# Counting TensorE's instruction blocks in a kernel's planning layer, and other PSUM buffers for two blocks of a projection

## The chip, the core and the metric

The kernel runs on one core of a Trainium2 chip. A core has a matrix engine (TensorE, PE in the profile, its weight loads PEld), a vector engine (DVE), a scalar engine (ACT), GpSimd (POOL) and SyncE (SP), which here only issues transfers. The engines run side by side, each through its own list of instructions in order, and wait for one another by semaphores. Matrix products land in PSUM; everything else lives in SBUF. The metric is the device time of one execution in microseconds.

## The reference

One decoder layer for 512 tokens of width 1024, in float32. The input is RMS-normed and projected; the projection is cut into three groups of heads, whose outputs are merged by one output projection, and a SwiGLU block follows. The change lies in the projection and in the second group, a gated linear recurrence (HGRN2):

```python
h = rmsnorm(x, norm_mix[l])
proj = h @ w_in[l]
c_q, c_kv, k_rope, hq, hf, hi, hg, mq = [proj[..., offsets[j]:offsets[j + 1]] for j in range(len(IN_SIZES))]
...
q = jax.nn.silu(q_raw.astype(f32)) * (HG_DK ** -0.5)
f = lbf + (1.0 - lbf) * jax.nn.sigmoid(f_raw.astype(f32))
k = 1.0 - f
...
x = x + (mix @ w_out[l]).astype(x.dtype)
h2 = rmsnorm(x, norm_ffn[l])
x = x + ((jax.nn.silu(h2 @ w_gate[l]) * (h2 @ w_up[l])) @ w_down[l]).astype(x.dtype)
```

## The kernel before

**Products in three passes.** An operand is split into a rounded high part and the rest (`split`, L487: ACT makes `hi`, DVE makes `lo`), and `mm3` (L517) sums three matmuls, high by high, high by low, low by high. Each of the three is one weight load and one matmul in the fp32r type: two instructions in TensorE's list. Weights come by transfer into a raw tile `wr` (three of them, `load`, L495) and are split by `piece` (L502) into `wh` and `wl` (five and four tiles).

**The order is planned.** `body` (L409) does not issue instructions; it records them with a `Recorder` (L47). `price` (L185) gives each one an estimated duration in ns. `run` (L242) then simulates the five engines: it takes again and again the operation that can start first (ties by priority), notes its end, releases what waited for it, and keeps the order in which it took them. A few copies and memsets may go to either of two engines, and `run` picks the one that ends first. `issue` (L363) emits the recorded operations in that order, with no times in it. So a price changes the order of instructions and the choice of an engine for some of them, and nothing else: on the chip each engine runs its list as soon as its semaphores allow.

**PSUM buffers.** A buffer is one bank of 128x512 float32: three are named `mm`, three `at`, two `tr`. A new product takes a buffer of its name that is free, and its first matmul waits, if it must, until the buffer's last reader is done.

**The stretch around the change.** `hg_in(h)` (L712) for heads 0 to 3 calls `gated` (L701) twice, for projection blocks 5+h and 9+h: `feat` (L624) sums 8 x 3 matmuls of 128x512, then DVE multiplies by `RX` (the norm's factor, spread over a tile; z) and ACT takes the sigmoid. Blocks 5 and 9 have their weights early and are computed interleaved, as pieces of the input arrive; blocks 6, 10, 7, 11, 8 and 12 follow with weights from `wr`. `RX` exists only when all of x has arrived and its squares have been summed. Then come the value projections (`wide`, L727, with `wva` and `wvb`), and between their matmuls the intra-chunk scores of the recurrence, in `hg_levels` (L776): a first `scores` (L783) on the raw q and k, then one per level m = 1, 2, 4, 8, 16, each after DVE has multiplied q, k and the totals up a level (`step_up`, L831), and each masked into a tile by `copy_predicated` (`put`, L793). One `scores` is 64 matmuls of a 32x32 corner of the array in plain float32; TensorE runs each as two loads and two matmuls, so 256 instructions of a few ns each. In the trace these are the instructions of L380; all others are of L383. The q and k of level m are written over in place once `scores` has read them.

Later stretches: the latent attention and the memory attention, the output projection, and the SwiGLU block in three column groups.

Of the kernel before, what the change touches and what calls it, by code (L numbers as in the profile page):

```python
# [9 lines left out]
F32R = mybir.dt.float32r  # L10
I32 = mybir.dt.int32
U8 = mybir.dt.uint8
AF = mybir.ActivationFunctionType
# [33 lines left out]
class Recorder:  # L47
# [137 lines left out]
    def price(self, o, outs, ins):  # L185
        n = max(self._free(a) for a in outs)
        if o.name == "dma_start":
            return 1000 if o.eng == "gpsimd" else 475
        if o.eng == "tensor":
            if o.name == "tiles":  # L190
                return 270 + 2.1 * sum(max(35, self._free(p[2])) for p in o.kw["parts"]) / len({self._rng(p[0])[2] for p in o.kw["parts"]})
            if o.name == "transpose":
                return 109.5
            if ins[0].dtype == F32R:
                return n / 2.4 + (15.5 if n >= 512 else 14) if n >= 256 else max(1.67 * n, 107)
            return 222 if n <= 2 else 64 if n <= 32 else 122 if n <= 64 else 226 if n <= 128 else 436 if n <= 256 else 1.7 * n
        m = max([self._free(a) for a in ins] + [n])
        fast = self.inside(ins)
        if o.eng == "scalar":
            fn = o.args[2] if o.name == "activation" else None  # L200
            if fn is not None:
                o.table = self.TABLES.get(str(fn).split(".")[-1])
            return (92 if fast else 45) + 0.835 * m + (190 if "accum_out" in o.kw else 0) + (100 if hasattr(o.kw.get("scale"), "ap") else 0)
        if o.eng == "vector":
            if o.name == "reciprocal":
                return 70 + 6.6 * m
            if o.name == "tensor_copy":
                return 66 + (0.55 if fast else 1.045) * m
            if o.name == "tensor_scalar":
                return 66 + (0.62 if fast else 1.045) * m + 60 * any(hasattr(a, "ap") for a in o.args[2:])  # L210
            if o.name == "memset":
                return 60 + 0.5 * m
            if o.name == "scalar_tensor_tensor":
                return 68 + 1.15 * m
            return 68 + 1.045 * m
        if o.name == "memset":
            return 40 + m * 0.8
        if o.name == "tensor_scalar":
            return 244 + 0.84 * m
        return 170 + 2.17 * m  # L220

    def shares(self, o, outs, ins):
# [12 lines left out]
        ("scalar", "scalar"): 135, ("scalar", "vector"): 140, ("scalar", "tensor"): 202, ("scalar", "gpsimd"): 200, ("scalar", "sync"): 130,  # L235
        ("gpsimd", "gpsimd"): 105, ("gpsimd", "vector"): 75, ("gpsimd", "scalar"): 75, ("gpsimd", "tensor"): 215, ("gpsimd", "sync"): 130,
    }


    IDLE = (1500, 3400)  # L240

    def run(self):  # L242
# [18 lines left out]
                    cand[e].append(o)  # L261
        table, dma, done, out, port, cold = None, 0.0, 0, [], 0.0, 0.0
        busy = {e: 0.0 for e in engs}
        while done < len(ops):
            best = None
            for e in engs:
                be = None
                for o in cand[e]:
                    t = max(free[e], o.ready)
                    if o.alts[e][5]:  # L270
                        t = max(t, port)
                    ok = True
                    if o.new:
                        need = {}
                        for k in o.new:
# [12 lines left out]
                            t = max(t, sorted(free_)[skip + j])  # L288
# [3 lines left out]
                    t = max(t, free[e])  # L292
# [33 lines left out]
            if o.eng == "tensor":  # L326
                if t - free["tensor"] > self.IDLE[0] or not free["tensor"]:
                    cold = t + self.IDLE[1]
                slow = min(2 * cost, max(0.0, cold - t))
                cost += slow / 2  # L330
            end = t + cost
            if both:
                port = end
# [2 lines left out]
            if o.dma:  # L336
                ap = o.kw["out"]
# [71 lines left out]
def body(ctx, tc, t):  # L409
# [14 lines left out]
    def nm(p):  # L424
        cnt[0] += 1
        return f"{p}_{cnt[0]}"
# [6 lines left out]
    def sb(tag, shape=(P, S), dt=F32):  # L433
        return rec.tile("SB", shape, dt, tag, nm(tag), BUFS[tag])

    def ps(tag, bufs, shape=(P, S)):
        return rec.tile("PS", shape, F32, tag, nm(tag), bufs)

    def ps_mm():
        return ps("mm", BUFS["mm"])  # L440

    def ps_at():
        return ps("at", BUFS["at"])

    def ps_tr():
        return ps("tr", BUFS["tr"])
# [28 lines left out]
    with rec.first(0):  # L475

        o = rec.tile("PS", (P, S), F32, "tr", nm("tr"), BUFS["tr"])
# [17 lines left out]
    def load(src, n=1024):  # L495

        raw = sb("wr", (P, 1024))
        with rec.first(0):
            DMA.dma_start(out=raw[:, :n], in_=src)
        return raw  # L500
# [43 lines left out]
    def colsums(sqs, nblk=NB, more=None):  # L544

        o = ps_ts()[:, 0:2 * nblk * len(sqs)]
        ks = [(i, b) for i in range(len(sqs)) for b in range(nblk)]
        v = o.rearrange("p (i b two) -> p i b two", two=2, b=nblk)
        T.tiles(o, ones, *sqs, parts=[
            (v[g:g + 32, i, b], sqs[i][:, b * P + g:b * P + g + 32], ones, (i, b) == ks[0], (i, b) == ks[-1] and more is None)  # L550
            for i, b in ks for g in range(0, P, 32)
        ])
        if more is not None:
            T.tiles(o, ones, more, parts=[
                (v[g:g + 32, 0, b], more[:, b * P + g:b * P + g + 32], ones, False, b == nblk - 1)
                for b in range(nblk) for g in range(0, P, 32)
            ])
        return v[..., 0]
# [27 lines left out]
    with rec.first(0):  # L586
# [6 lines left out]
        for k in range(KD):  # L593

            if k in EARLY:
                n, tag = EARLY[k]
# [9 lines left out]
        for k in range(KD):  # L606
            if k in EARLY:
                n = EARLY[k][0]
# [15 lines left out]
    def feat(dst, raw, acts):  # L624

        if isinstance(raw, list):
            w = raw.__getitem__
        else:
            w = pieces(raw)
        for k in range(KD):  # L630
            mm3(dst, w(k), acts[k], k == 0, k == KD - 1)
# [68 lines left out]

    def gated(i):  # L701

        o = ps_mm()
        feat(o, early[i // 9] if i in (5, 9) else load(t["wf"][i]), xg)
        z = sb("td")
        s_ = sb("td")
        with rec.first(0):
            V.tensor_tensor(z, o, RX, ALU.mult)
            A.activation(s_, z, AF.Sigmoid)
        return z, s_  # L710

    def hg_in(h):  # L712
        with rec.first(2):
            z, s_ = gated(5 + h)
            q = f(spots.pop(0))
            with rec.first(0):
                V.scalar_tensor_tensor(q, z, 128 ** -0.5, s_, ALU.mult, ALU.mult)
            z, s_ = gated(9 + h)
            fg = f(spots.pop(0))
            k_ = sb("tm")  # L720
            with rec.first(0):
                A.activation(fg, s_, AF.Identity, bias=lb[:, h:h + 1], scale=omlb[:, h:h + 1])
                A.activation(k_, fg, AF.Identity, bias=ones[:, 0:1], scale=-1.0)
                V.tensor_scalar(fg, fg, 1.0, None, ALU.min)
        return q, k_, fg
# [145 lines left out]
    def hg_gate(h, y):  # L871
        with rec.first(2):
            z, s_ = gated(13 + h)
        V.tensor_tensor(z, z, s_, ALU.mult)
        V.tensor_tensor(y, y, z, ALU.mult)
# [65 lines left out]
    with rec.first(0):  # L941
        o = colsums([cq_sq, ckv_sq])
# [25 lines left out]
    for h in range(4):  # L968
        o = ps_mm()
# [11 lines left out]
    for b in range(NB):  # L981
        o = ps_mm()[:, :256]
# [3 lines left out]
        o = o.rearrange("p (h d) -> p h d", h=4)  # L986
# [44 lines left out]
    for i in range(2):  # L1031
        w = [piece(r, i * S, (i + 1) * S) for r in wukv]
        for b in range(NB):
            o = ps_mm()
# [69 lines left out]
    def rope_t(src):  # L1104

        o = ps_tr()
        for b in range(NB):
            T.transpose(o[:, b * P:(b + 1) * P], src[:, b].rearrange("p a b -> p (a b)"), ident)
        return o

    ym = []
    for h in range(4):
# [6 lines left out]
        if h % 2 == 0:  # L1119
            o = rope_t(qr[:, :, h:h + 2, :])  # L1120
# [12 lines left out]
        for g in range(2):  # L1133
            pb = []
            for b in (2 * g, 2 * g + 1):
# [3 lines left out]
                o = ps_at()  # L1139
# [34 lines left out]
    for h in range(4):  # L1174
        o = ps_mm()
# [19 lines left out]
    for h in range(4):  # L1195
# [6 lines left out]
        for g in range(2):  # L1202
            pb = []
            for b in (2 * g, 2 * g + 1):
                bs = slice(b * P, (b + 1) * P)
                o = ps_at()
# [9 lines left out]
    with rec.first(2):  # L1216
        for i in range(KD):
            y = sb("tm")
            DMA.dma_start(out=y, in_=t["xT"][:, i * S:(i + 1) * S])
            o = ps_mm()  # L1220
# [12 lines left out]
    o = ps_tr()  # L1233
# [7 lines left out]
    for i in X_ORDER:  # L1241
        o = ps_mm()
# [54 lines left out]
    o = ps_tr()  # L1297
# [101 lines left out]
    for c0, w in FF:  # L1399
# [16 lines left out]
        for j in range(2 * w // P):  # L1416
            g, js = (cu[0:2] + cu[4:6], j * P) if j < w // P else (cu[2:4] + cu[6:8], j * P - w)
            hi, lo = sb("mx" if last else "xh", dt=F32R), sb("y" if last else "xl", dt=F32R)
            with rec.first(0):
                o = ps_tr()  # L1420
# [100 lines left out]
```

## Time and profile before

| what | value |
|---|---|
| median of 3 runs | 711.58 us (710.45 to 711.79) |
| the profiled execution's own time | 709.22 us |
| its span, first to last instruction | 707.4 us |
| mean granted TensorE clock | 1.000 of full speed |
| busy: PE, DVE, ACT, POOL | 688.6, 546.7, 375.3, 92.8 us |

Start times count from the start of the span. A line of the timeline gives start, duration, engine, source line, operation, output<-inputs, the number of merged instructions, and in brackets the idle time of the engine before it with what ended it; "issue" means that the profile shows nothing that it waited for. The ends of matmuls are modelled: the next one starts before the shown end. A few per cent of the matmul records may be missing.

### The profile page before, as it was taken

How to read it: one execution, taken by the hardware profiler on the slowest of the kernel's cores; microseconds unless marked ns; L12 is line 12 of the kernel's file. 1: busy time of each engine (PE TensorE's matmuls, PEld its weight loads, DVE VectorE, ACT ScalarE, POOL GpSimd, SP SyncE). 2: the span in 40 equal slices, each digit the busy share in tenths (PEclk: the TensorE clock that was granted, in tenths of full speed). 3: DMA queues.
4: the chain of work that ended last, by engine and by line, in shares of the span. 5: the costliest groups of instructions: out<-in, count | busy, mean ns of one | idle time of the engine just before them, and what ended most of it. 6: DMA issues, size and time to landing. Idle time of an engine off the chain costs nothing.

```text
span 707.4 us, 12975 instructions
## 1 busy us (share of the span) xinstructions
PE 688.6 (97%) x4755; PEld 574.1 (81%) x4755; DVE 546.7 (77%) x1234; ACT 375.3 (53%) x721; POOL 92.8 (13%) x124
## 2 busy tenths in 40 slices
PE   8998899999999999999999998999999999999997
PEld 6787877887888877887878786888888899999886
DVE  7986799779989989888999769656549767548732
ACT  7763245447587654664776553645543365544420
POOL 1000000000000000000323442023112312310000
PEclk9999999999999999999999999999999999999999
DMA  8522221113333323215999899779957848941251
GB/s 284 161 66 91 84 63 46 31 63 120 89 120 120 118 65 101 75 31 183 281 278 226 182 244 218 191 164 219 212 127 184 162 130 193 225 87 34 68 146 62
DMA packets 47727, 98.04 MB, mean 139 GB/s; under 512 B 5424, under 2 KB 15536, under 8 KB 47664
## 3 DMA queue, kind: packets, MB, share of 16 engines
q1 hardware_dynamic: 33408, 73.62, 32.3%
q0 software_dynamic: 13824, 23.07, 20.4%
q8 instruction: 37, 0.61, 0.3%
q10 hardware_dynamic: 432, 0.53, 0.2%
q14 instruction: 26, 0.21, 0.1%
HBM read 95.11 MB, written 2.10 MB: 137 GB/s over the span
## 4 chain that ended last, share of the span: by engine, by line
PE 86%; DVE 6%; issue 3%; DMA 3%; ACT 2%; ACTq 0%; POOL 0%; DVEq 0%; POOLq 0%
PE mm L383 43%; PE tr L383 21%; PE at L383 20%; DMA xl<-in_wg 2%; DVE wl L383 2%; PE at L380 1%; DMA tc<-in_we 1%; DVE hd L383 1%; PE tr L380 1%; ACT wh L383 0%; DVE ptl L383 0%; DVE td L383 0%; DVE qr L383 0%; ACT hd L383 0%; DVE tm L383 0%
## 5 line engine op out<-in xcount | busy, mean ns | idle before, releaser
L383 ACT CAST wh<-wr 128x512 fp32r<-128x512 f32 (+2 forms) x141 | 84.0, 599 | 101.0 <-PE tr L383 44.4
L383 DVE TENSOR_TENSOR wl<-wr,wh 128x512 fp32r<-128x512 f32 (+2 forms) x148 | 96.9, 658 | 33.9 <-issue 11.6
L383 PE MATMUL mm<-xh,wh 128*128 128x512 f32 x248 | 98.0, 398 | 2.0 <-DVE td L383 1.5
L383 PE MATMUL mm<-xh,wl 128*128 128x512 f32 x248 | 98.4, 397 | 0.0
L383 PE MATMUL mm<-xl,wh 128*128 128x512 f32 x248 | 98.1, 396 | 0.1
L383 DVE TENSOR_TENSOR wl<-y,wh 128x512 fp32r<-128x512 f32 (+1 forms) x84 | 53.4, 638 | 41.8 <-PE tr L383 19.3
L383 ACT CAST wh<-y 128x512 fp32r<-128x512 f32 (+1 forms) x82 | 47.4, 581 | 65.9 <-PE at L383 35.5
L383 DVE TENSOR_TENSOR wl<-mx,wh 128x512 fp32r<-128x512 f32 (+1 forms) x72 | 46.1, 645 | 33.5 <-PE tr L383 14.8
L383 PE MATMUL mm<-wh,hd 128*128 128x512 f32 (+2 forms) x176 | 59.7, 366 | 0.7 <-ACT wh L383 0.7
L383 ACT CAST wh<-mx 128x512 fp32r<-128x512 f32 (+1 forms) x67 | 39.0, 585 | 37.2 <-PE at L383 17.7
L383 PEld LDWEIGHTS mm<-xh,wh 128*128 128x128 f32 x248 | 46.6, 188 | 11.5 <-DVE td L383 1.8
L383 PEld LDWEIGHTS mm<-xl,wh 128*128 128x128 f32 x248 | 46.6, 188 | 9.9 <-DVE xl L383 1.0
L383 PEld LDWEIGHTS mm<-xh,wl 128*128 128x128 f32 x248 | 46.7, 188 | 9.0 <-DVE wl L383 0.4
L383 POOL DMA_DIRECT2D y<-in_wu x36 | 32.2, 955 | 104.4 <-DVE wl L383 77.2
L383 PE MATMUL at<-wh,hd 128*128 128x512 f32 (+1 forms) x120 | 45.0, 375 | 0.0
L383 PE MATMUL tr<-xl,wh 128*128 128x512 f32 x112 | 43.8, 391 | 0.0
L383 PE MATMUL tr<-xh,wl 128*128 128x512 f32 x112 | 43.7, 390 | 0.0
L383 PE MATMUL tr<-xh,wh 128*128 128x512 f32 x112 | 43.7, 390 | 0.0
L383 PEld LDWEIGHTS mm<-wh,hd 128*128 128x128 f32 x176 | 32.3, 188 | 5.8 <-ACT wh L383 1.1
L383 PE MATMUL mm<-wh,v 128*128 128x512 f32 (+1 forms) x96 | 35.8, 375 | 0.0
L383 PE MATMUL at<-wh,v 128*128 128x512 f32 (+1 forms) x96 | 35.8, 375 | 0.0
L383 PE MATMUL mm<-wl,hd 128*128 128x512 f32 (+2 forms) x88 | 32.5, 369 | 0.4 <-DVE wl L383 0.4
(409 smaller groups left out, 1676.9 us busy)
## 6 DMA issues: line engine op xcount, KB each, us to landing
wr<-in_wf SPq DMA_DIRECT2D x19, 512.0 KB, 3.4
wr<-in_wd SPq DMA_DIRECT2D x16, 512.0 KB, 4.7
mx<-in_wg SPq DMA_DIRECT2D x24, 256.0 KB, 5.4
mx<-in_wu SPq DMA_DIRECT2D x24, 256.0 KB, 5.7
y<-in_wu POOLq DMA_DIRECT2D x24, 256.0 KB, 6.3
tm<-in_xT SPq DMA_DIRECT2D x16, 256.0 KB, 4.5
wr<-in_wt SPq DMA_DIRECT2D x8, 512.0 KB, 3.8
wr<-in_wo SPq DMA_DIRECT2D x8, 512.0 KB, 3.6
```

Source lines behind the costliest of these rows:

```text
L380: r = self.nc.tensor.matmul(get(a), lhsT=get(b), rhs=get(c), start=first, stop=last, skip_group_check=True)
L383: r = getattr(getattr(self.nc, o.eng), o.name)(*[get(a) for a in o.args], **{k: get(a) for k, a in o.kw.items()})
```

## The change

In `price`, three estimates go up: an ACT activation with the function Identity by 90 ns, a `scalar_tensor_tensor` on DVE whose scalar is a tensor by 35 ns, and `copy_predicated` from 68 to 118 ns plus the same slope. In `run`, the simulated TensorE counts its instructions (`length`: 4 for each part of a `scores`-like operation and for a plain float32 matmul, 2 for the others), starting at 63; whenever the count passes a multiple of 256, the crossing may not come earlier than 5200 ns after the previous one began, and the operation is made longer by what is missing. In `gated`, blocks 5 and 9 take an `at` buffer instead of an `mm` buffer.

```diff
@@ price
-            return (92 if fast else 45) + 0.835 * m + (190 if "accum_out" in o.kw else 0) + (100 if hasattr(o.kw.get("scale"), "ap") else 0)
+            return (92 if fast else 45) + 0.835 * m + 90 * (fn == AF.Identity) + (190 if "accum_out" in o.kw else 0) + (100 if hasattr(o.kw.get("scale"), "ap") else 0)
...
             if o.name == "scalar_tensor_tensor":
-                return 68 + 1.15 * m
+                return 68 + 1.15 * m + 35 * hasattr(o.args[2], "ap")
+            if o.name == "copy_predicated":
+                return 118 + 1.045 * m
             return 68 + 1.045 * m
@@ Recorder
+    FETCH, BLOCK, AHEAD = 5200, 256, 63
+
+    def length(self, o):
+
+        if o.name == "tiles":
+            return 4 * len(o.kw["parts"])
+        return 2 if o.name == "transpose" or o.kw["rhs"].dtype == F32R else 4
@@ run
+        begun, count = -1e9, self.AHEAD
...
                 slow = min(2 * cost, max(0.0, cold - t))
                 cost += slow / 2
+                n, full = self.length(o), cost
+                count += n
+                for b in range((count - n) // self.BLOCK + 1, count // self.BLOCK + 1):
+                    at = t + cost - full * (count - self.BLOCK * b) / n
+                    cost += max(0.0, begun + self.FETCH - at)
+                    begun = max(at, begun + self.FETCH)
             end = t + cost
@@ gated
-        o = ps_mm()
+        o = ps_at() if i in (5, 9) else ps_mm()
```

## Rows read from the trace of the kernel before

**Rows 1.** The page: the span, and TensorE's line of busy time and instructions.
```profile
span 707.4 us, 12975 instructions
PE 688.6 (97%) x4755; PEld 574.1 (81%) x4755; DVE 546.7 (77%) x1234; ACT 375.3 (53%) x721; POOL 92.8 (13%) x124
```

**Rows 2.** Busy time by 10 us windows: window, length, then each engine's busy time (instructions).
```profile
20.00:30.00 10.00, 8.54 (x70) 6.51 (x69) 8.59 (x33) 6.43 (x9) 0.00 (x0) 1.00 0.68 217
...
60.00:70.00 10.00, 7.11 (x245) 6.57 (x245) 6.84 (x17) 1.70 (x3) 0.00 (x0) 1.00 0.29 95
...
80.00:90.00 10.00, 8.41 (x303) 7.95 (x302) 6.19 (x18) 1.25 (x2) 0.00 (x0) 1.00 0.23 82
...
430.00:440.00 10.00, 7.75 (x35) 5.37 (x35) 10.00 (x17) 2.84 (x6) 2.54 (x4) 1.00 1.06 268
...
700.00:710.00 10.00, 3.52 (x16) 2.59 (x14) 0.93 (x3) 0.00 (x0) 0.00 (x0) 0.95 0.14 52
```

**Rows 3.** Waits of TensorE: line, releaser, us in total, times, longest.
```profile
PE at L380 <- issue: 4.5, 2, 2.9
...
PE mm L383 <- DVE td L383: 1.5, 1, 1.5
PE at L380 <- DVE tm L383: 1.1, 2, 0.8
```

**Rows 4.** Timeline of PE and DVE around the wait at 25 us, and a later split.
```profile
24.73 0.47 PE L383 MATMUL mm<-xh,wl 128*128 128x512 f32 x1
...
25.31 0.69 DVE L383 TENSOR_TENSOR wl<-wr,wh 128x512 fp32r<-128x512 f32 x1 [0.86 <-PE mm L383]
25.92 1.28 DVE L383 TENSOR_TENSOR td<-mm,RX 128x512 f32<-128x512 f32 x2
...
26.66 0.50 PE L383 MATMUL mm<-xh,wh 128*128 128x512 f32 x1 [1.46 <-DVE td L383]
...
44.53 0.68 DVE L383 TENSOR_TENSOR wl<-wr,wh 128x512 fp32r<-128x512 f32 x1
```

**Rows 5.** The chain that ended last, four pieces: start, us, what.
```profile
26.66 28.37 PE mm L383 x126
...
58.55 1.23 PE at L380 x82
59.77 0.93 PE tr L383 x5
...
83.91 0.71 PE mm L383 x6
```

**Rows 6.** Timeline around four of the `scores` operations.
```profile
60.64 0.86 PE L380 MATMUL at<-y,tm 128*32 128x32 f32 x76
...
64.39 0.65 PE L380 MATMUL at<-y,tm 128*32 128x32 f32 x52 [2.89 <-issue]
...
65.09 0.74 DVE L383 COPY_PREDICATED tc<-lmask,at 128x512 f32<-128x512 uint8 x1 [2.71 <-PE at L380]
...
80.37 1.13 PE L380 MATMUL at<-y,tm 128*32 128x32 f32 x108
83.09 0.38 PE L380 MATMUL at<-y,tm 128*32 128x32 f32 x20 [1.59 <-issue]
...
88.27 1.30 PE L380 MATMUL at<-y,tm 128*32 128x32 f32 x128
```

**Rows 7.** Busy time and instructions between the two waits marked issue, columns as in rows 2.
```profile
61.57:81.57 20.00, 16.89 (x383) 15.98 (x382) 14.57 (x39) 5.70 (x11) 0.00 (x0) 1.00 0.26 84
```

**Rows 8.** DMA queues: one of the two that carry instructions (packets, MB, share).
```profile
q8 instruction: 37, 0.61, 0.3%
```

**Rows 9.** Groups of DVE and ACT instructions whose price changes: busy us, mean ns.
```profile
L383 DVE SCALAR_TENSOR_TENSOR xl<-tm,p,xh 128x512 fp32r<-128x512 f32 x8 | 5.8, 751 | 0.4 <-ACT xh L383 0.4
...
L383 DVE COPY_PREDICATED tc<-lmask,at 128x512 f32<-128x512 uint8 x5 | 3.7, 740 | 7.4 <-PE at L380 7.4
...
L383 ACT ACTIVATE tm<-pth,ones 128x512 f32<-128x512 f32 x2 | 1.4, 716 | 0.0
```

## The prediction, made before the changed kernel ran

> **What bounds the kernel now.** I read the page's busy times first: TensorE is busy 688.6 of 707.4 us [rows 1], so no edit that leaves its matmuls alone can win more than the 18.8 us in which it stands still. Then the busy times by windows of 10 us, to see where it stands: 1.46 us are missing between 20 and 30, 2.89 between 60 and 70, 1.59 between 80 and 90, 2.25 between 430 and 440, and in the last window 3.88 of the 7.4 us that are left of the span [rows 2]. What is over lies in small pieces and in the first 10 us. Then TensorE's waits, for their names: 4.5 us in two waits at `scores` for which the profile shows no releaser, 1.5 us in one wait of a projection block for DVE, 1.1 us for the recurrence's k [rows 3]. The change touches only these three; the reader should see that they come to 7.1 us.
>
> **The 1.46 us at 25 us** is a PSUM wait. TensorE has issued its last matmul of the third block at 24.73 and starts the fourth at 26.66, released by the first z of DVE (the two z's start at 25.92) [rows 4]. z is the only reader of the `mm` buffer of block 5, and the fourth block needs that buffer: blocks 5, 9 and 6 hold all three. z cannot come earlier, since it waits for the norm.
>
> **The two waits without a releaser** look like instruction supply. Queue 8 moved 0.61 MB in 37 packets [rows 8]; TensorE's list has 4755 + 4755 instructions [rows 1], which is 257 for each packet and 64 bytes for each instruction. The second wait comes 383 + 382 = 765 recorded instructions after the first [rows 7], and three blocks of 256 are 768. Both fall inside a `scores`, after 76 and after 108 of its 128 matmuls [rows 6], where 256 instructions pass in 1.30 us (the undisturbed one at 88.27 [rows 6]). How long does a block take to come? Before the second wait, 2 x 108 = 216 instructions of the `scores` had run; the boundary before lay 40 instructions, 20 matmuls, ahead of it, at 0.71 / 6 = 0.12 us each [rows 5]: at 80.37 - 2.4 = 77.97. TensorE went on at 83.09, so 5.1 us. Before the first, 152 had run, and 5 matmuls (10 instructions) lie between it and the `scores` before [rows 5, 6]; so the boundary before lay 94 instructions ahead of the end of that one (59.77, 128 matmuls in about 1.25 us): near 59.3, and 64.39 - 59.3 = 5.1 us again. A block is asked for when the one before begins, and needs 5.1 us; that costs nothing where 256 instructions take longer, as they do in ordinary matmuls (128 of 0.12 us are 15 us).
>
> By the Trainium skill (Runtime: NRT & Kernel Launch, Instruction fetch mechanics) crossing a block is "one DMA tail-bump, mostly hidden". The trace agrees for most crossings and contradicts it for these two; what the time would be by the page is the last rival below.
>
> **The buffers, step by step.** With blocks 5 and 9 in `at`, the three `mm` buffers are free for the next three blocks, and the fourth block waits for no z. Its weights are there: six pieces precede it, and the DVE split at 25.31 is of the fifth block's second half, 1.5 blocks (36 matmuls of 28.37 / 126 = 0.225 us [rows 5], 8.1 us) before it is needed. So TensorE goes on at 24.73 + 0.23 = 24.96 instead of 26.66: between 1.46 (the idle time shown) and 1.70 us; I take 1.5. Does it keep them? From 26.66 the chain is TensorE alone for 28.37 us [rows 5]. The last weight split of the six loaded blocks is done at 44.53 + 0.68 = 45.2 [rows 4] and is needed 108 matmuls after 26.66, at 51.0: 5.8 us to spare, more than 1.7. The `at` buffers are next wanted at 58.5 [rows 5], 31 us after both z's. Nothing queues behind a new wait. Low bound: 0, if the shift turns into waiting for DVE at the later levels, where the 1.1 us [rows 3] show that it is just in time.
>
> **Counting blocks.** This adds no instruction. It does not move the stall away by itself: `run` takes the operation that can start first whether or not it will be stalled, it only learns that it ends late. `scores` of level 1 follows the first one within 0.9 us, in the new order as in the old, because both want the same k; so the first stall stays at about 2.9 us. Its bounds: 0 if enough matmuls come between, and 5.1 - 1.3 = 3.8 if none do, so -2.9 to +0.9. The other four levels (m = 2, 4, 8, 16) are a lottery on where the boundary falls. A `scores` is stalled if the boundary before it lies fewer than k instructions ahead, with 0.06 k + 1.3 - 0.005 k < 5.1, k < 69: a quarter of the positions, up to 3.8 us and on average 1.9. Now one of the four is hit (1.59); the expectation is 4 x 0.27 x 1.9 = 2.0. I take no difference, bounds -1.6 and +3.8.
>
> **What the plan gains from knowing.** During the first stall DVE stands still 2.71 us [rows 6], which the old plan did not foresee; a plan that does may put a weight split there, which helps where DVE is late by 1.1 us in all [rows 3]. I take half, -0.5; bounds 0 and -1.1, or +1 if work put there delays the masking.
>
> **Prices.** The three reprices move instructions only by their order. Rows hold for Identity (716 ns) and `copy_predicated` (740) [rows 9]; the tensor-scalar form at 512 is shown with 751 ns, 11 above `copy_predicated` [rows 9], and is now priced 39 above it (692 against 653), so that edit overshoots by some 30 ns. These are 50 to 90 ns on some 50 instructions; what covers them is that DVE and ACT are off the chain. Their cost is that the order of everything after 30 us may change, which is not computed here: of such waits the 2.25 us at 430 are the largest [rows 2], and I allow plus and minus 2.
>
> **Sum.** -1.5 + 0 + 0 - 0.5 = -2.0 us. The profiled execution took 709.22 us, 1.8 over its span, and becomes 707.2; it stands 2.36 us below the median, so on the median's scale I predict 709.6. A measurement of this kernel tells about 0.2%, 1.4 us, from no change; so the forecast lies just past that line, and its own range, from a lottery of about 1.2 us, is 708.2 to 711.0.
>
> **Rivals.**
> *Given back at the levels:* the 1.5 us arrive, but DVE's level chain does not move and TensorE waits for it there instead, or the lottery draws one stall more. For: it is already 1.1 us late there; against: DVE's own idle time there is mostly waiting for TensorE. -2.0 + 1.5 = -0.5: 711.1.
> *The stalls go:* the new order puts the boundary elsewhere, the 1.59 vanishes and the first shrinks by half: -2.0 - 1.6 - 1.4 = -5.0: 706.6. For: any shift by 30 more instructions before the level at 80.37 is enough; against: the first two `scores` stay neighbours.
> *Slower, by the boundary:* the reordered list lets two of the levels m = 2 to 16 start with the boundary fewer than about 30 instructions ahead, each stalled by 5.1 - 1.3 - 0.055 x 15 = 3.0 us; against 1.59 now that is +4.4, and DVE, held by each, gives nothing back: -1.5 + 4.4 = +2.9: 714.5. It decides at k = 69, and from the second hit on the kernel is no faster.
> *Nothing to count:* the two waits are not block supply, and the plan now inserts up to 3.8 us after `scores` that the chip does not have. DVE work put before a masking by mistake makes the chain of levels late, by about the 2.7 us that it believes idle: -1.5 + 2.7 = +1.2: 712.8. The 765 recorded instructions speak against it. The hidden refill of the Trainium skill (the page and section named above) would make it so.
>
> **Chances.** Forecast 0.40; given back 0.22; the stalls go 0.18; slower by the boundary 0.15; nothing to count 0.05. Faster by over 0.2%: the third and most of the first (0.36), 0.54. Within 0.2% (710.2 to 713.0): the rest of the first, the second less a little, the last, 0.28. Slower: 0.18. The range 705.8 to 713.4 leaves out a little at the far side of *the stalls go* and most of *slower by the boundary*.
>
> **What would show it.** In the changed profile the wait of a projection block for td should be gone and the fourth block start near 25.0; a wait marked issue of about 2.9 us should stand in the level-1 `scores`, near 60; every stalled `scores` should have its previous boundary less than 69 instructions ahead, and the wait end 5.1 us after that boundary. The forecast is wrong if TensorE waits at the levels for DVE by over 2 us, or if a new wait of over 1 us stands after 120 us.

## The result, and the profile after

The changed kernel takes 707.38 us (median of 5 runs, 706.17 to 709.14) against 711.79 (710.45 to 712.30) for the kernel before in the same runs: ratio 0.9942, 95% interval 0.9921 to 0.9962. The forecast of 709.6 had the sign. The measured time lies in the whole range of the prediction, 705.8 to 713.4, but below the 708.2 to 711.0 that it gave to the forecast itself, and nearer to the rival *the stalls go* (706.6); the gain of 4.4 us is about twice the 2.0 of its sum.

The profiled execution took 708.16 us. The page of the changed kernel, its span and the busy times, against [rows 1]:

```profile
span 706.4 us, 12989 instructions
PE 691.2 (98%) x4755; PEld 579.2 (82%) x4755; DVE 544.8 (77%) x1224; ACT 381.9 (54%) x733; POOL 93.0 (13%) x124
```

TensorE's waits in the changed kernel, against [rows 3]. L399 holds the `scores`, L402 all the rest:

```profile
PE at L399 <- issue: 2.9, 1, 2.9
PE tr L402 <- DVE ptl L402: 2.4, 2, 2.2
PE tr L402 <- DVE ones_r L402: 2.0, 1, 2.0
PE at L399 <- DVE tm L402: 1.1, 2, 0.8
```

The wait of a projection block for td is gone, and so is one of the two waits marked issue; the longer one is there as before, with the same 2.9 us. The two lines between are not new; in the kernel before they read:

```profile
PE tr L383 <- DVE ones_r L383: 2.0, 1, 2.0
PE tr L383 <- DVE ptl L383: 2.0, 2, 1.7
```

Both signs that would have shown the forecast wrong stayed away: TensorE waits 1.1 us for DVE at the levels, and no new wait of over 1 us stands after 120 us. Busy time by 10 us windows of the changed kernel, columns as in [rows 2], to be read against the same windows there:

```profile
20.00:30.00 10.00, 10.00 (x78) 7.97 (x77) 9.10 (x33) 6.44 (x9) 0.00 (x0) 1.00 0.65 191
...
60.00:70.00 10.00, 7.61 (x97) 7.35 (x101) 4.93 (x13) 1.70 (x3) 0.00 (x0) 0.66 0.16 48
...
80.00:90.00 10.00, 10.00 (x318) 9.65 (x317) 7.20 (x21) 1.56 (x3) 0.00 (x0) 1.00 0.33 108
...
430.00:440.00 10.00, 7.45 (x30) 5.39 (x29) 10.00 (x17) 3.24 (x7) 4.38 (x5) 0.83 0.96 221
```

From 20 to 30 and from 80 to 90 TensorE is now busy throughout. But look at the clock column, the first number behind the engines: 0.66 from 60 to 70, 0.83 from 430 to 440, where [rows 2] show 1.00. The profiled execution of before never ran at half clock, and this one did so twice. That is why the two profiled executions, 708.16 and 709.22 us, lie closer together than the medians.

Timeline of TensorE in the changed kernel around the `scores` of level 1, against [rows 6]:

```profile
58.64 0.86 PE L399 MATMUL at<-y,tm 128*32 128x32 f32 x76
62.40 0.96 PE L399 MATMUL at<-y,tm 128*32 128x32 f32 x52 [2.89 <-issue]
...
64.52 0.47 PE L402 MATMUL mm<-wh,xh 128*128 128x320 f32 x1
...
64.78 0.47 PE L402 MATMUL mm<-wl,xh 128*128 128x320 f32 x1
...
81.14 1.30 PE L399 MATMUL at<-y,tm 128*32 128x32 f32 x128
```

Level 1 starts at 58.64 instead of 60.64, so the 1.5 us of the buffers have arrived and half a microsecond more. It stops after the same 76 matmuls. What follows runs at half clock until 68.0, and level 4 (81.14) runs its 128 matmuls through. The chain that ended last shows the stop as a link of its own, between two links of `scores`:

```profile
58.71 0.79 PE at L399 x56
59.50 2.89 issue
62.40 0.96 PE at L399 x52
```

On this chain nothing else fills those 2.89 us.

### The profile page after: what moved, and what is told of

Same layout as the page of the kernel before. It is cut to its first block, busy times and chain, and to the rows that moved or that the text cites. A ratio compares the mean times of both kernels' runs of the same rounds, so it can differ in the third digit from the quotient of the medians.

```text
span 706.4 us, 12989 instructions
## 1 busy us (share of the span) xinstructions
PE 691.2 (98%) x4755; PEld 579.2 (82%) x4755; DVE 544.8 (77%) x1224; ACT 381.9 (54%) x733; POOL 93.0 (13%) x124
## 4 chain that ended last, share of the span: by engine, by line
PE 90%; DVE 6%; ACT 2%; DMA 1%; issue 1%; ACTq 0%; DVEq 0%
PE mm L402 45%; PE at L402 22%; PE tr L402 21%; PE at L399 1%; DVE hd L402 1%; DVE wl L402 1%; DMA tc<-in_we 1%; PE tr L399 1%; DVE ptl L402 1%; ACT wh L402 1%; DVE tm L402 1%; DVE y L402 0%; ACT hd L402 0%; DVE qr L402 0%; DVE td L402 0%
## 5 line engine op out<-in xcount | busy, mean ns | idle before, releaser
L402 ACT CAST wh<-wr 128x512 fp32r<-128x512 f32 (+2 forms) x140 | 83.2, 597 | 97.6 <-PE tr L402 45.1
L402 DVE TENSOR_TENSOR wl<-wr,wh 128x512 fp32r<-128x512 f32 (+2 forms) x148 | 96.7, 656 | 32.6 <-issue 12.5
L402 PE MATMUL mm<-xh,wl 128*128 128x512 f32 x232 | 92.2, 398 | 0.0
L402 PE MATMUL mm<-xl,wh 128*128 128x512 f32 x232 | 92.0, 397 | 0.0
L402 PE MATMUL mm<-xh,wh 128*128 128x512 f32 x232 | 91.2, 394 | 0.0
L402 DVE TENSOR_TENSOR wl<-y,wh 128x512 fp32r<-128x512 f32 (+1 forms) x84 | 52.9, 636 | 42.9 <-PE tr L402 19.3
L402 ACT CAST wh<-y 128x512 fp32r<-128x512 f32 (+1 forms) x79 | 45.7, 579 | 66.3 <-PE at L402 34.8
L402 DVE TENSOR_TENSOR wl<-mx,wh 128x512 fp32r<-128x512 f32 (+1 forms) x72 | 45.8, 642 | 32.3 <-PE tr L402 15.1
L402 ACT CAST wh<-mx 128x512 fp32r<-128x512 f32 (+1 forms) x69 | 40.1, 584 | 42.3 <-PE at L402 22.9
L402 PE MATMUL mm<-wh,hd 128*128 128x512 f32 (+2 forms) x176 | 59.9, 367 | 1.0 <-ACT wh L402 1.0
L402 PEld LDWEIGHTS mm<-xl,wh 128*128 128x128 f32 x232 | 43.6, 188 | 8.6
L402 PEld LDWEIGHTS mm<-xh,wh 128*128 128x128 f32 x232 | 43.6, 188 | 8.0
L402 PEld LDWEIGHTS mm<-xh,wl 128*128 128x128 f32 x232 | 43.7, 188 | 7.9
L402 POOL DMA_DIRECT2D y<-in_wu x36 | 32.9, 938 | 100.3 <-DVE wl L402 71.5
L402 PE MATMUL at<-wh,hd 128*128 128x512 f32 (+1 forms) x120 | 45.0, 377 | 0.0
L402 PE MATMUL tr<-xl,wh 128*128 128x512 f32 x112 | 43.8, 391 | 0.0
L402 PE MATMUL tr<-xh,wl 128*128 128x512 f32 x112 | 43.7, 390 | 0.0
L402 PE MATMUL tr<-xh,wh 128*128 128x512 f32 x112 | 43.7, 390 | 0.0
L402 PEld LDWEIGHTS mm<-wh,hd 128*128 128x128 f32 x176 | 32.5, 189 | 6.1 <-ACT wh L402 1.8
L402 PE MATMUL mm<-wh,v 128*128 128x512 f32 (+1 forms) x96 | 36.2, 377 | 0.0
L402 PE MATMUL at<-wh,v 128*128 128x512 f32 (+1 forms) x96 | 35.6, 372 | 0.0
L402 PE MATMUL mm<-wl,hd 128*128 128x512 f32 (+2 forms) x88 | 32.7, 372 | 0.2 <-DVE wl L402 0.2
```

Source lines behind the costliest of these rows:

```text
L402: r = getattr(getattr(self.nc, o.eng), o.name)(*[get(a) for a in o.args], **{k: get(a) for k, a in o.kw.items()})
```

## The experiments

Each kernel is one of the two with the edit shown. Ratios are to the kernel before, run on the same chip. As each execution lists its mean granted clock, there is a second reading. The 35 executions of before that ran beside the first four kernels took 709.10 us on average at clock 1.000 (4 of them), 710.52 at 0.998 (11), 711.88 at 0.995 (12) and 713.60 at 0.993 (8): 4.5 / 7 = 0.64 us for each 0.001 of mean clock. An **estimate at full clock** takes that off each run of a kernel, and the median of these is given: 709.0 to 709.1 for before, 704.3 for the changed kernel, so -4.8. It separates what an edit does to the work from how often the clock fell. It is rough: the slope is that of the kernel before, the runs of other kernels alone give slopes from 0.36 (e4) to 0.80 (e7), and e4 and e7 have no run above a clock of 0.996, so their estimates can be off by one to two microseconds.

**e1: the buffers alone**, the first of four that part the change.

```diff
-        o = ps_mm()
+        o = ps_at() if i in (5, 9) else ps_mm()
```

> Only the two PSUM buffers are changed; prices and planning are those of before. Theory A (the gain has parts that add: the buffer wait at 25 us, and the second supply wait at 81 us): TensorE's wait for td near 25 us is gone, level 1 starts 1.5 to 2.0 us earlier than 60.64, both waits marked issue stay (2.9 and 1.6 us), because the boundary lies 40 instructions ahead of the m=4 scores as before; the time falls by 1.5 to 2.0 us, ratio 0.9975. Rival B (what the buffer gives is waited for again at the levels): the time stays within 0.7 us, ratio 0.999 to 1.001.

Measured 0.9963 [0.9942, 0.9984], 710.06 us. The four runs at clock 1.000 average 707.54, against 709.10: -1.6. The wait for td is gone, and both waits marked issue are there (4.7 us in two). Level 1 starts at 59.54, 1.1 us earlier than before and not the 1.5 to 2.0 expected, but the time gained is what the sum had: this term was right in size and in place.

**e2: the three prices alone.**

```diff
+ 90 * (fn == AF.Identity)
+ 35 * hasattr(o.args[2], "ap")
+            if o.name == "copy_predicated":
+                return 118 + 1.045 * m
```

> Only the three prices are changed; buffers are those of before and no block is counted. Theory A: the wait of 1.5 us at 25 us stays; the prices move the weight transfers against the levels, so that the second supply wait (1.6 us at 81) goes; the time falls by 1.0 to 2.0 us, ratio 0.998. Rival C (prices of 35 to 90 ns only shuffle work that is hidden): ratio 0.999 to 1.001.

Measured 1.0018 [0.9996, 1.0041], 713.12 us. One of the two issue waits is gone (3.3 us in one; before, 4.5 in two), and the kernel is no faster all the same. At full clock the estimate is 709.0, no change. So a vanished wait is not a gain by itself; that the new order costs as much elsewhere follows from this estimate alone and was not traced to an operation.

**e3: the counting alone.** `price` and `gated` as before, `length` and the lines in `run` as in the change.

> Only the counting of blocks is added; buffers and prices are those of before. Theory A: up to the last level the list of TensorE has the same positions against the blocks as before, so all three waits stay; ratio 0.999 to 1.001. Rival D (the counting is what gives the gain, by placing DVE work into the stalls): ratio below 0.997.

Measured 1.0000 [0.9979, 1.0021], 711.61 us; two issue waits, 4.0 us. The wait that the plan now knows of is not avoided, as the prediction had it, and the plan gains nothing from knowing. TensorE's instructions, read in order from the two traces, are those of the kernel before up to 186 us.

**e4: everything but the counting.**

```diff
-                    cost += max(0.0, begun + self.FETCH - at)
+                    cost += 0.0
```

> Prices and buffers as in the changed kernel, but no counting of blocks. Theory A: the two gains add, no wait at 25 us, only one wait marked issue; the ratio is that of the whole change, 0.994 (0.993 to 0.996). Rival D: it stays at 0.997 or above, and the rest belongs to the counting.

Measured 0.9996 [0.9979, 1.0013], 711.41 us, with a single issue wait of 2.9 us and none for td. TensorE's list is that of the changed kernel up to 104 us, so over the last level of the `scores`, which starts at 96.79 here and at 96.31 in the changed kernel. Expected was the ratio of the whole change, 0.994; that is refuted. Both profiled executions ran at half clock in the same two stretches, and they end 3.8 us apart (spans 710.2 and 706.4). TensorE's waits between 96 and 364 us, first of e4, then of the changed kernel:

```profile
PE at L399 <- DVE tm L402: 1.0, 2, 0.6
PE mm L402 <- ACT wh L402: 0.7, 1, 0.7
PE mm L402 <- DVE xl L402: 0.7, 1, 0.7
PE tr L402 <- ACT tm L402: 0.5, 1, 0.5
PE at L402 <- DVE tm L402: 0.5, 1, 0.5
PE mm L402 <- ACT td L402: 0.4, 1, 0.4
PE tr L402 <- DVE y L402: 0.4, 1, 0.4
PE tr L399 <- DVE y L402: 0.2, 1, 0.2
```

```profile
PE at L399 <- DVE tm L402: 1.1, 2, 0.8
PE mm L402 <- ACT wh L402: 0.7, 1, 0.7
PE at L402 <- DVE tm L402: 0.5, 2, 0.4
PE tr L402 <- ACT tm L402: 0.3, 1, 0.3
```

4.4 us against 2.6: four short waits for DVE and ACT (xl, td and twice y) that the other order does not have. That names 1.8 of the 3.8 us; half a microsecond lies before the last level, and the rest is not named. So what counting gives in the full change comes mostly after the last `scores`, in the order of what follows it.

**e5: buffers and counting; e6: prices and counting; e7 and e8: the full change with a wrong model** (e7: the boundaries half a block off; e8: a block taken for slower than it is). If the plan gains because it knows the blocks, counting should help in every company and a wrong model should not.

```diff
e5: the three edits of price are left out
e6
-        o = ps_at() if i in (5, 9) else ps_mm()
+        o = ps_mm()
e7
-    FETCH, BLOCK, AHEAD = 5200, 256, 63
+    FETCH, BLOCK, AHEAD = 5200, 256, 191
e8
+    FETCH, BLOCK, AHEAD = 8000, 256, 63
```

> Buffers and counting as in the changed kernel, prices of before. Theory K (a plan that knows the stalls is better wherever they are): counting gives again what it gave on top of prices and buffers, 0.9942 against 0.9996; so 0.9963 of the buffers alone less 0.005, about 0.991. Theory L (counting only draws another order after the last level; good or bad by chance): near the buffers alone, 0.996, give or take 0.002, since on the prices of before counting alone changed nothing (1.000).

> Prices and counting as in the changed kernel, blocks 5 and 9 in the mm buffers as before. Both theories: the whole change less the buffers; the wait of 1.5 us for td near 25 us is back and the time is 1.5 to 2.5 us above the changed kernel: ratio to before 0.9965 (0.995 to 0.998). If it is at 0.994, the buffers give nothing in this order.

> The changed kernel with the count started at 191 instead of 63, so the planned block boundaries lie half a block away from the real ones; TensorE's list before the levels is the same. Theory K (right knowledge of the boundaries gives the gain): the gain of counting is lost or turned round, ratio at 0.999 or above, as without counting (0.9996). Theory L (any change of the plan draws a new order): anywhere from 0.993 to 1.001; a ratio under 0.997 refutes K.

> The changed kernel with 8000 ns for a block instead of 5200, against 5.1 us shown by the two waits. Theory K: the plan now foresees stalls that are 2.8 us too long; it is worse than with 5200 by some part of what counting gave, 0.996 to 1.000. Theory L: anywhere from 0.993 to 1.001, with no tie to how true the figure is.

| kernel | ratio [95%] | median us | mean clock of its runs | at full clock, estimate against before |
|---|---|---|---|---|
| e1 buffers | 0.9963 [0.9942, 0.9984] | 710.06 | 0.9965 | -1.7 |
| e2 prices | 1.0018 [0.9996, 1.0041] | 713.12 | 0.9935 | 0 |
| e3 counting | 1.0000 [0.9979, 1.0021] | 711.61 | 0.9971 | +0.6 |
| e4 prices, buffers | 0.9996 [0.9979, 1.0013] | 711.41 | 0.9934 | -2.1 |
| e5 buffers, counting | 1.0014 [0.9995, 1.0034] | 712.19 | 0.9946 | -0.4 |
| e6 prices, counting | 0.9974 [0.9957, 0.9991] | 709.04 | 0.9957 | -2.4 |
| all three (the change) | 0.9942 [0.9921, 0.9962] | 707.38 | 0.9950 | -4.8 |
| e7 all, boundaries off | 1.0021 [1.0003, 1.0039] | 712.61 | 0.9929 | -0.9 |
| e8 all, 8000 ns | 0.9986 [0.9969, 1.0003] | 710.73 | 0.9943 | -2.1 |

Read down by what counting adds: 1.0000 alone; with the buffers it takes their gain away (e1 to e5, +0.5%); with the prices it gains 0.44% (e2 to e6); with both, 0.54% (e4 to the change). An edit whose effect changes sign with its company is acting through the order that comes out of it. e5 speaks most clearly against a plan that gains by knowing: that was to give 0.991. It lies above the 0.996 of the other theory too. That e7 and e8 lose most of the gain fits both readings, since they too are other orders, and e6 and the change, the two that gain, both have the new prices: that true figures help in that company is not excluded. In e7 level 4 stops again, by 2.51 us.

**e9: where a block ends.** Twenty tiny matmuls (40 instructions) behind the first ten matmuls, in the kernel before.

```diff
+                for i in range(20):
+                    r = self.nc.tensor.matmul(get(o.args[0])[:, 0, 0:2], lhsT=get(o.kw["lhsT"]), rhs=get(o.kw["lhsT"])[:, 0:2], start=True, stop=True)
```

> The kernel before with 20 tiny matmuls (40 instructions) added at the head of TensorE's list and nothing else moved. If the waits marked issue are boundaries of 256 instructions, every boundary falls 40 instructions earlier: the level-1 scores stops after 56 of its 128 matmuls instead of 76; the m=4 scores, now 81 instructions after a boundary instead of 41, does not stop at all; and the m=16 scores, 7 instructions after one, stops for 1.7 to 3.4 us after some 124 matmuls, where before it ran through. If the waits belong to the scores themselves or to what they read, they stay at 76 and 108 matmuls. The time is not the point: up to 2 us for the added matmuls at the start.

Measured 1.0040 [1.0020, 1.0060], 715.06 us. Timeline of TensorE in e9, the `scores` of levels 1, 4 and 16, to be read against [rows 6]:

```profile
67.12 0.82 PE L400 MATMUL at<-y,tm 128*32 128x32 f32 x72 [3.05 <-issue]
...
84.80 0.96 PE L400 MATMUL at<-y,tm 128*32 128x32 f32 x88
87.71 0.56 PE L400 MATMUL at<-y,tm 128*32 128x32 f32 x40 [1.95 <-issue]
...
102.17 1.30 PE L400 MATMUL at<-y,tm 128*32 128x32 f32 x128
```

The stops come after 128 - 72 = 56 and after 88 matmuls, where before they came after 76 and 108 [rows 6]: both 20 matmuls earlier. The wait is tied to a count of TensorE's instructions (256, by the working from [rows 1] and [rows 7]) and to nothing that those matmuls read. But its length is not: level 4 stopped though it should have been clear of its boundary, and level 16 ran through though it should not. A fixed time per block fails here. For level 16 the DMA queues of e9 show an instruction packet from 100.5 to 100.7 us, before it began:

```profile
q8 instruction: 1, 0.02, 32.1%
```

So either the boundary counted for it is off, or a block can be asked for earlier than at the start of the one before; the runs do not tell which.

**e10: two weight transfers held back**, in the kernel before: those issued at 58.63 and 77.83 us there, close to the two boundaries that hurt (59.2 and about 77.9). They now follow the masking of levels 1 and 4, behind a one-column memset that holds them there; TensorE's list is the same.

```diff
+LATE = {("in_wvb", 2): 1, ("in_wf", 9): 3}
...
+            if o.name == "copy_predicated":
+                puts += 1
+                if puts in late:
+                    q = late.pop(puts)
+                    r = self.nc.vector.memset(get(q.kw["out"])[:, 0:1], 0.0)
...
+                    r = self.nc.sync.dma_start(**{k: get(a) for k, a in q.kw.items()})
```

> The kernel before with two weight transfers of 512 KB held back: the second of wvb until the level-1 masking, the ninth of wf until the m=4 masking (a DVE memset of one column after the masking, which the transfer must wait for). Theory Q (the instruction packet waits behind the weight packets on the DMA engines; without them a block comes in about 3.4 us: 1.4 to the packet, 1.0 for it, 1.0 after it): the wait in the level-1 scores falls from 2.9 to about 1.2 us and the one at m=4 from 1.6 to 0. Theory F (a block takes 5.1 us whatever the DMA does): both stay. By Q the time falls by 2 to 4 us, ratio 0.995 to 0.998, unless TensorE has to wait for the late weights.

Measured 0.9949 [0.9931, 0.9968], 708.03 us. Timeline of e10, TensorE, levels 1 and 4:

```profile
62.49 0.65 PE L406 MATMUL at<-y,tm 128*32 128x32 f32 x52 [0.86 <-issue]
...
79.86 0.38 PE L406 MATMUL at<-y,tm 128*32 128x32 f32 x20 [0.23 <-issue]
```

The same stops at the same matmuls, 0.86 and 0.23 us instead of 2.89 and 1.59 (expected were 1.2 and 0). The two profiled executions, both at full clock, took 706.22 and 709.22: 3.4 us of stops are gone and 3.0 us of time. The medians lie 4.0 us apart, in part because the clock fell less often (mean 0.998 against 0.996); the estimate at full clock is -2.6. So the edit is worth more than the buffers either way. The issue of the transfer on SP's timeline, and the instruction packet in narrow windows of the DMA queues, tell why. First the kernel before, and its queue 8 from 62.0 to 62.2 us (packets, MB, share of 16 engines):

```profile
58.63 0.33 SPq L383 DMA_DIRECT2D wr<-in_wvb  x1
```

```profile
q8 instruction: 1, 0.02, 29.6%
```

Then e10, the issue of the same transfer, and queue 8 from 60.0 to 60.2 us:

```profile
64.01 0.33 SPq L417 DMA_DIRECT2D wr<-in_wvb  x1
```

```profile
q8 instruction: 1, 0.02, 30.4%
```

The boundary is crossed at 59.2 and 59.3 (counted back from the stop, as in the prediction). Before, the packet comes at 62.1, when the 512 KB are through; in e10, where nothing is on the way, at 60.1. From the packet to TensorE's next matmul it is 2.3 us in the one (64.39) and 2.4 in the other (62.49). So this block took 3.2 us with no weights on the way, and 5.2 behind a transfer of 512 KB. At the second stop of e10, counted back in the same way, it took some 3.9 us (boundary near 76.0, packet at 77.5, TensorE at 79.86), against 5.3 before.

**e11: the same hold in the changed kernel; e12: the changed kernel with the first two `scores` pulled apart**, their heads 0 to 2 issued earlier, between ordinary matmuls, so that 256 instructions no longer pass in 1.3 us.

```diff
e12
+            for group in early.get(n, []):
+                for a, b, c, first, last in group:
+                    r = self.nc.tensor.matmul(get(a), lhsT=get(b), rhs=get(c), start=first, stop=last, skip_group_check=True)
...
-                for a, b, c, first, last in o.kw["parts"]:
+                for a, b, c, first, last in own.get(n, o.kw["parts"]):
```

> The same two transfers held back in the changed kernel. Theory Q: its one wait marked issue falls from 2.9 to about 1.2 us, and with it the chance of the half clock that follows it; ratio to before 0.990 to 0.993. Theory F: as the changed kernel, 0.994.

> The changed kernel with the first two scores taken apart by head: the parts of heads 0 to 2 are issued earlier on TensorE, 12 matmuls after their operands, so that no 256 small instructions follow one another there; all other instructions keep their order, and the counts from level m=2 on are the same. Both theories: no wait marked issue near 60, no half clock after it; 2.9 us of standing still and up to 3 us of half clock go; ratio to before 0.988 (0.985 to 0.991). If it is 0.993 or above, the wait was hidden by the chain of levels on DVE.

e11 measured 0.9897 [0.9880, 0.9913], 704.57 us (703.57 to 705.00 in 4 runs), and beats both kernels. e12 measured 0.9915 [0.9901, 0.9928], 705.74 us, short of the 0.985 to 0.991 that was expected. At full clock the estimates are -5.7 and -5.2, against -4.8 for the changed kernel: most of what e11 and e12 gain over it comes from the clock, whose mean is 0.998 and 0.997 against 0.995, and about 0.9 and 0.4 us from the work. TensorE in the `scores` of level 1, first of e11, then of e12:

```profile
60.80 0.66 PE L406 MATMUL at<-y,tm 128*32 128x32 f32 x52 [1.05 <-issue]
```

```profile
62.70 0.46 PE L418 MATMUL at<-y,tm 128*32 128x32 f32 x32 [0.78 <-DVE y L421]
```

In e11 1.84 us of the stop are gone. In e12 all of it is, but the last head then waits 0.78 us for DVE's y, and the pieces cost time themselves: the same 410 matmuls, from the projection at 25.4 us to the end of level 1, take 35.98 us in e11 and 37.60 in e12, so 34.9 and 36.8 without these waits. The 1.9 us between them are the larger part of what e12 lacks.

## Why the prediction was right, and where not

**The buffers: right.** Predicted -1.5, with e1 measuring -1.6 in its runs at full clock. The step "TensorE goes on at 24.73 + 0.23 = 24.96" can be read in the changed kernel, matmuls of TensorE and the two z's of DVE:

```profile
24.87 0.48 PE L402 MATMUL mm<-xl,wh 128*128 128x512 f32 x1
25.18 0.39 PE L402 MATMUL mm<-xh,wl 128*128 128x512 f32 x1
...
25.77 1.29 DVE L402 TENSOR_TENSOR td<-at,RX 128x512 f32<-128x512 f32 x2 [0.45 <-ACT RX L402]
```

TensorE goes through while the z's are still to come.

**Counting moves no stall away by itself: right**, by e3, and in the changed kernel the first one stayed at 2.9.

**What the plan gains from knowing: wrong in kind.** The -0.5 was argued from knowledge: DVE's 2.71 us at the first stop were to be filled. In the changed kernel DVE stands still as long there, 3.04 us:

```profile
63.40 0.73 DVE L402 COPY_PREDICATED tc<-lmask,at 128x512 f32<-128x512 uint8 x1 [3.04 <-PE at L399]
```

By e3 to e6 counting is worth +0.6, +1.3, -2.4 and -2.7 us at full clock, in company of nothing, the buffers, the prices and both: differences of the last column above. TensorE's list first differs behind the last `scores` (at 104 us from e4 to the change, at 186 from before to e3), so no product was moved into a stop either. It is another draw of the order; why this draw was a good one is open.

**The prices: zero alone, not zero in company.** The step "I allow plus and minus 2" was applied to them by themselves, and e2 gives 0. The change is -4.8 at full clock where its parts alone add up to -1.7 + 0 + 0.6 = -1.1. This is the term that was mis-sized: one order's effect was put at 0 with a width of 2 for the prices and 1.2 for counting, and the order of both together is worth -3.7. The estimates are rough, but the measured ratios say the same: the parts add up to -0.2%, the change is -0.6%. So the sign came from the buffers, for the reason given, and the rest of the gain from no term of the sum: that part was luck.

**Of the rivals, "the stalls go" came half true.** The 1.59 vanished and the first stop did not shrink. But the reason given for it, "any shift by 30 more instructions before the level at 80.37 is enough", is not what happened. Counted back over the list, level 4 of the changed kernel starts 48 instructions after a boundary; before it was 41, and both are below the 69 that were to decide. What changed is when SP issued the weights of that stretch: at the boundary in the kernel before (near 77.9), half a microsecond behind it (78.5) in the changed kernel. The issue in the one and in the other:

```profile
77.83 0.33 SPq L383 DMA_DIRECT2D wr<-in_wf  x1
```

```profile
78.99 6.00 SPq L402 DMA_DIRECT2D wr<-in_wf  x2
```

The DMA queues of the changed kernel from 78.0 to 80.5 us, in 40 slices, with the instruction packet as the lone 9 in the middle and the weights only after it:

```profile
DMA  0000000000000000000000090000000097903018
...
q8 instruction: 1, 0.02, 2.5%
```

**"A block is asked for when the one before begins, and needs 5.1 us": right for the two stalls it was fitted to, wrong as a rule.** Both lay behind a 512 KB transfer. e10 shows 3.2 and 3.9 us without one, and e9 a third value: the boundary there was crossed at 79.0, and the packet came only at 85.4. So k = 69 is not a property of the kernel. TensorE goes on 2.2 to 2.4 us after the packet, and when the packet comes depends, among other things, on what SP sent just before.

**The half clock was in no step.** The profiled execution of before had none of it, so no row could show its cost. In the changed kernel's profiled execution it slowed the stretch from 61.2 to 68.0, where one 128x320 matmul starts 0.26 us after another (64.52 and 64.78, above), while six of them take 0.88 us, 0.147 each, in the chain of before:

```profile
65.39 0.88 PE mm L383 x6
```

Level 2 starts at 69.86, against 69.28 before, although level 1 had started 2.0 us earlier. Against e11, which has the same list of TensorE and ran at full clock here, the stretch from level 1 to level 2 took 11.22 us instead of 6.96, of which 1.84 are the longer stop: so 2.4 us were lost there, in this execution.

**Open:** why the packet of e9 came some 6 us after its boundary. The DMA queues of e9 from 78 to 86 us, in 40 slices of 0.2, show one weight transfer end near 80, then about 3 us with next to nothing on the way, then a second transfer, and the packet only behind that:

```profile
DMA  3964979992010000000000000096797898920300
```

So weights ahead of the packet are not the whole of it. Open too: which operations of the combined order give the last 3.7 us, beyond the short waits of e4, and how often the clock falls in which order, which decided the medians of e2, e4 and e7 as much as the work did.

## What to carry to other kernels

A run of tiny matmuls uses up TensorE's instruction block faster than the next one comes, and the price of that depends on the transfers in flight: keep large ones out of the microseconds around it before teaching a planner to count. Spreading the tiny matmuls among large ones removed the stop too, but cost 1.9 us of its own here. An edit to a planner's prices must be measured in the company in which it will run, since its effect passes through one new order of everything. And compare executions at the same mean granted clock, or a fraction of a per cent cannot be told from how often the clock fell.

## What the runs showed of the hardware

**Instruction blocks share the transfer engines.** The packet, 16 KB by [rows 8], takes 0.95 us of one transfer engine (29.6% of 16 over 0.2 us); TensorE goes on 2.2 to 2.4 us after it appears, in before, the changed kernel, e9 and e10 alike. With no weights on the way it appears 0.8 and 1.5 us after the boundary, at the two stops of e10; behind one transfer of 512 KB 2.7 to 3.1, in before, the changed kernel and the first stop of e9; and 6.4 us after it at the second stop of e9, with the gap shown above. The Trainium skill (Runtime: NRT & Kernel Launch, Instruction fetch mechanics) has blocks of 256 instructions and a crossing that is mostly hidden. e9 agrees with the blocks. Two crossings cost 4.5 us in the kernel before, and holding back two transfers gave 0.5%, about a third of it, by the estimate, through the clock.

**TensorE's granted clock falls after some stops.** Windows of 1 us in the changed kernel, the clock being the third number from the end:

```profile
61.00:62.00 1.00, 0.00 (x0) 0.00 (x0) 0.00 (x0) 0.00 (x0) 0.00 (x0) 0.60 0.00 0
62.00:63.00 1.00, 0.60 (x44) 0.61 (x48) 0.00 (x0) 0.00 (x0) 0.00 (x0) 0.50 0.00 0
...
68.00:69.00 1.00, 1.00 (x8) 1.00 (x8) 0.80 (x3) 0.00 (x0) 0.00 (x0) 0.99 0.50 82
```

The stop of 2.89 us begins at 59.5; the clock falls to half, 1.2 of its two levels 1.2 and 2.4 GHz, at about 61.2, still within the stop, and is back at 68.0. The second fall, at 436.7, follows the 2.16 us in which TensorE waited for ptl. The kernel before has a stop of the same 2.89 us and one of 1.74 for ptl, and ran at full clock throughout in its profiled execution; of its 35 executions beside e1 to e4, 31 show a mean clock below 1.000. So the same stop sometimes costs its own length and sometimes more, and most of this kernel's spread, 709 to 714 us between the averages at clock 1.000 and 0.993, goes with the clock.
